# The mLSTM's queries held once per direction in tiles of 128 rows, with zeros in the other direction's half

## The chip, the cores and the metric

The kernel runs on one core of a Trainium2 chip. The metric is the device time of one execution in microseconds (us), lower is better, as the median of several executions. A profile of one execution gives the span from its first to its last instruction and what each engine did: TensorE (PE for its matmuls, PEld for its weight loads), VectorE (DVE), ScalarE (ACT), GpSimd (POOL), and SyncE's queue (SPq), which issues the transfers.

## The reference, cut to what matters

Two layers of a hybrid backbone run over 512 latent and 256 context tokens of 1024 features. In each layer a modulated RMSNorm feeds one input projection, and three mixers work side by side on it: a bidirectional mLSTM, grouped attention and a bidirectional gated delta net. Their outputs are gated, summed and projected, and a gated MLP follows. The change is in the mLSTM, which for each of 4 heads (64 features of q and k, 128 of v), for each direction and for chunks of tokens computes

```
s   = (q k^T) * exp(dlog - mt)                 within the chunk
num = s v + e_inter * (q C)                    C: the state before the chunk, [64, 128]
den = sum(s) + e_inter * (q n)                 n: [64]
h   = num / max(|den|, exp(-mt))
C, n <- decay * (C, n) + sum_s wk[s] k[s] (v[s], 1)
```

with q scaled by 64 ** -0.5 = 0.125. The forward and the backward h are added, normed over the head and gated. The last layer needs only the latent tokens.

## The kernel before

Tokens stand in six tiles of 128 (0 to 3 latent, 4 and 5 context); a tile is a chunk of the mLSTM. The tile framework of the kernel orders each engine's instructions by priorities and a timeline simulation, hands out slots of on-chip memory by tag (a tag has a fixed number of slots; a new tile of the tag waits until an old one is no longer read), and puts in all waits. `PLAN` names the order in which the parts of a layer are traced and their priorities: `P0`, `P1` and `g0`, `g1` are the delta net's projections and scans, `qp`, `ga` the attention, `mp` the mLSTM's projections, `ml` the mLSTM itself (function `mlstm`), and `mg` the gates of the merge, which are large products. In both layers `ml` is traced after `g1` and before `mg`; TensorE takes instructions of `g1`, `ml`, `mg` and of the modulation (`adp`, L467, 32 columns of the array) in turns, in one fixed sequence.

`gates` computes all decay factors. `X[:, 0]` are the factors e_inter; they are copied to `R2` (L839) and written as rows to DRAM, from where `row_bc` (L854) broadcasts rows over partitions.

`mlstm` has two parts. The first makes the states `U` of all tiles: rows 0 to 63 hold the forward direction's 64 features, rows 64 to 127 the backward direction's. The second, from L963 on, goes over the tiles (six in layer 0, four in layer 1), for each:

- `kT` (L964), 64 rows, and `qd` (L968), 128 rows with the same queries in both halves, are loaded from DRAM; both take slots of tag `b2`, which has seven and also serves `mb` (twice a tile) and `v`.
- `psS` (L972) is k times q for four heads, with 64 rows of the array.
- For each direction `mb` is loaded (L854), turned into decay weights (DVE L979, ACT L981) and multiplied by `psS` (DVE L982).
- `qd` is multiplied by 0.125 and by `e2`, the rows e_inter of the forward direction in the upper half and of the backward direction in the lower (L988, one DVE instruction over 128 x 512).
- For each pair of heads, direction and head a product with all 128 rows (L1002: decay weights times v) opens the sum in PSUM, and a product with 64 rows (L1004) adds the state's part. The forward direction uses rows 0 to 63 and the backward direction rows 64 to 127 of `qd` and `U`. The first tile of a direction has no state and no L1004.
- L1010 to L1037 divide, add the directions, norm, turn and gate, and store the tile as `m0y` or `m1y`; on GpSimd run `rsqrt` (L183) and L1035 there, and the memset of a column of `v` (L918).

An f32 product is two instructions (passes) on TensorE: layer 0 has 6 x 2 x 4 - 8 = 40 products of L1004 and layer 1 has 4 x 2 x 4 = 32. `merge` takes the delta net's output first, then the attention's, then the mLSTM's.

Of the kernel before, what the change touches and what calls it, by code (L numbers as in the profile page):

```python
# [13 lines left out]
ALU = mybir.AluOpType  # L14
AX = mybir.AxisListType

D = 1024
# [12 lines left out]
# columns of the input projection  # L30
# [5 lines left out]
# token tiles 0..3 are latent, 4 and 5 context; scan orders of the two directions  # L36
ORDER = ((4, 5, 0, 1, 2, 3), (5, 4, 3, 2, 1, 0))

# The mixers of each layer: the order in which their parts are traced, the priorities of the parts and of the weights
# (the long chains of small steps first, the large products in between), the PSUM of the context tokens in P1.  # L40
# P0, P1: projections of the delta net's pairs of heads, g0, g1: their scans; qp, ga: attention; mp, ml: mLSTM;
# cz, ao, mg: gates; n: from here on columns of the modulation in between.
# [51 lines left out]
class Kernel:  # L94
# [7 lines left out]
    # ---------------------------------------------------------------- pools  # L102
# [18 lines left out]
    # slots of the mixers' phase: a.. for the delta net, b.. for the others, gs for the projections  # L121
# [21 lines left out]
    # slots of the phase of the merge and the feed forward  # L143
# [12 lines left out]
    # PSUM banks: latent and context tokens of the large products, the delta net, the others  # L156
# [3 lines left out]
    def p0(self):  # L160
        """Banks of the latent tokens: those of the context tokens too where there are none."""
        self.turn = not self.turn
        return self.pb if self.spare and self.turn else self.pl
# [14 lines left out]
    # ---------------------------------------------------------------- small helpers  # L178
    def rsqrt(self, out, z, n, nm, who="n"):
        """out = z ** -0.5 for [128, n] float32 z (bit trick and Newton steps)."""  # L180
        nc = self.nc
# [18 lines left out]
    def split(self, h, l, x, eng=None):  # L200
        """x = h + l, both in float32r."""
# [5 lines left out]
    # ---------------------------------------------------------------- weights  # L207
    def wraw(self, src, nk, ncols, nm, slot=None):
        """raw weights [128, nk, ncols] from src rows (k p), columns given."""
# [17 lines left out]
    def gemm_fm(self, src, c0, ncols, nk, segs, done, nm):  # L227
        """Feature-major product: columns c0.. of src [nk*128, *] as stationary, tokens moving.
        segs: list of (token range, xh [128, nk, n], xl), latent first.
        done(block, [(psum, token range)]) takes the result."""  # L230
# [23 lines left out]
    def first_weights(self, src, c0, nk, nm, slot=None):  # L254
        """Weights for gemm_first."""
        h = l = None
# [879 lines left out]
    def attend_q(self, l, tt, tabs):  # L1136
# [7 lines left out]
        r = []  # L1144
# [769 lines left out]
```

## Time and profile before

| what | value |
|---|---|
| median of 3 runs | 2726.53 us (2725.04 to 2727.49) |
| span of the profiled execution | 2715.6 us, so that 10.9 us of the median lie outside the span |
| PE busy | 2663.0 us (98%) |
| DVE, ACT, POOL busy | 1573.4 us (58%), 998.5 us (37%), 235.0 us (9%) |
| chain that ended last | PE 88%, DMA 5%, DVE 3% |

No time other than the span is recorded for the profiled execution itself. A busy PE is not PE at its peak: the ends of matmuls are modelled, so the cost of a kind of product is read from the distance of starts, not from the busy time.

### The profile page before, as it was taken

To read this page: it belongs to the slowest core of one execution; us is meant where nothing else is said; L and a number is where in the kernel's file an instruction comes from. 1 tells how busy PE (TensorE), PEld (TensorE's weight loads), DVE (VectorE), ACT (ScalarE), POOL (GpSimd) and SP (SyncE) were. 2 spreads that over 40 slices of the span, in tenths; PEclk is the share of its full clock that TensorE was granted. 3 is DMA by queue.
4 is the path that set the end of the run, shared out by engine and by line. 5 is a ranking of instruction groups with operands and counts; after the bars stand their busy time and mean duration, and the time that the engine had idled before them with its cause. 6 is when DMAs were issued, how large, how long until landed. Compare 5 with 4: busy or idle time off the path is not lost.

```text
span 2715.6 us, 46016 instructions
## 1 busy us (share of the span) xinstructions
PE 2663.0 (98%) x18041; PEld 2261.6 (83%) x18041; DVE 1573.4 (58%) x3527; ACT 998.5 (37%) x2269; POOL 235.0 (9%) x234
## 2 busy tenths in 40 slices
PE   7999999999999999999999999999999999999999
PEld 5887988788888888888888899888877777888887
DVE  6775665756524655444444577867675646655555
ACT  5433354333322234232232254444633332433332
POOL 1000000000000410010010120000000003100000
PEclk9999999999999999999999999999998999999999
DMA  8354332556746423412212254422376675333332
GB/s 281 96 162 127 90 113 80 155 149 172 210 145 223 140 88 104 140 47 74 66 47 78 61 152 121 138 61 79 114 215 179 169 237 156 114 95 95 93 97 86
DMA packets 523466, 342.97 MB, mean 126 GB/s; under 512 B 48007, under 2 KB 488561, under 8 KB 522481
## 3 DMA queue, kind: packets, MB, share of 16 engines
q1 hardware_dynamic: 522961, 336.88, 42.2%
q8 instruction: 142, 2.33, 0.3%
q10 hardware_dynamic: 288, 3.15, 0.3%
q14 instruction: 75, 0.61, 0.1%
HBM read 283.92 MB, written 56.03 MB: 125 GB/s over the span
## 4 chain that ended last, share of the span: by engine, by line
PE 88%; DMA 5%; DVE 3%; ACT 1%; issue 1%; SPq 1%; POOL 0%; DVEq 0%; ACTq 0%; POOLq 0%
PE mg04p L249 2%; PE mg04p L250 2%; PE adp L467 2%; PE mg04p L248 2%; PE y0p L248 1%; PE y0p L250 1%; PE y0p L249 1%; PE mg14p L248 1%; PE mg14p L250 1%; PE mg14p L249 1%; PE y1p L248 1%; PE y0op L248 1%; PE y0op L250 1%; PE y0op L249 1%; PE y1p L249 1%
## 5 line engine op out<-in xcount | busy, mean ns | idle before, releaser
L1714 POOL TENSOR_TENSOR f0a<-f0a,f0g 128x768 f32<-128x768 f32 x22 | 40.7, 1848 | 486.8 <-DVE f0a L1702 486.8
L467 PE MATMUL adp<-ad,s 128*32 128x128 f32 x1280 | 65.5, 283 | 2.7 <-DVE cz0t L903 2.4
L1714 POOL TENSOR_TENSOR f1a<-f1a,f1g 128x512 f32<-128x512 f32 x22 | 28.5, 1294 | 315.4 <-DVE f1a L1702 284.4
L467 PEld LDWEIGHTS adp<-ad,s 128*32 128x32 f32 x1280 | 33.9, 110 | 26.0 <-issue 9.9
L1716 DVE TENSOR_TENSOR f0gl<-f0a,f0gh 128x768 fp32r<-128x768 f32 x22 | 21.1, 959 | 58.4 <-ACT f0gh L1715 58.4
L1715 ACT CAST f0gh<-f0a 128x768 fp32r<-128x768 f32 x22 | 18.3, 832 | 76.6 <-POOL f0a L1714 76.6
L1638 POOL TENSOR_TENSOR y0a<-y0a,y0g 128x768 f32<-128x768 f32 x16 | 33.0, 2062 | 129.9 <-DVE y0g L1635 127.6
L470 ACT COPY adr<-adp 128x128 f32<-128x128 f32 x80 | 21.2, 265 | 39.7 <-PE adp L467 39.3
L901 ACT ACTIVATE mg0t<-mg04p 128x512 f32<-128x512 f32 (+1 forms) x40 | 19.4, 486 | 38.5 <-PE mg04p L250 28.2
L1708 ACT ACTIVATE f0g<-f0g 128x768 f32<-128x768 f32 x22 | 18.5, 845 | 33.2 <-DVE f0g L1702 33.2
L1638 POOL TENSOR_TENSOR y1a<-y1a,y1g 128x512 f32<-128x512 f32 x16 | 23.9, 1494 | 78.3 <-DVE y1g L1635 78.3
L491 DVE TENSOR_REDUCE ada<-adc 128x2 f32<-128x8 f32 x80 | 12.9, 161 | 27.9 <-PE adc L489 27.6
L1635 DVE SCALAR_TENSOR_TENSOR y0g<-y0g,y0p 128x512 f32<-128x512 f32 (+1 forms) x32 | 17.4, 549 | 15.7 <-PE y0p L250 14.7
L1708 ACT ACTIVATE f1g<-f1g 128x512 f32<-128x512 f32 x22 | 13.8, 631 | 32.9 <-DVE f1g L1702 32.9
L979 DVE SCALAR_TENSOR_TENSOR m0mb<-m0mb,g0a,cst 128x128 f32<-128x128 f32 x48 | 14.0, 346 | 18.4 <-DMA m0mb<-g0rd 18.4
L489 PE MATMUL adc<-cst,adr 128*128 128x128 f32 x80 | 22.2, 278 | 0.4 <-ACT adr L470 0.4
L1659 DVE SCALAR_TENSOR_TENSOR hr<-y0op,y0gh,hr 128x512 f32<-128x512 f32 (+1 forms) x16 | 9.8, 615 | 21.0 <-PE y0op L250 21.0
L1002 PE MATMUL m0n<-m0vb,m0mb 128*128 128x129 f32 x96 | 19.1, 299 | 1.1 <-issue 1.1
L1611 DVE TENSOR_TENSOR y0l<-y0ld,y0h 128x768 fp32r<-128x768 f32 x12 | 13.0, 1093 | 12.2 <-ACT y0h L1610 12.2
L1734 DVE SCALAR_TENSOR_TENSOR hr<-f0d8p,ada,hr 128x512 f32<-128x512 f32 (+1 forms) x16 | 9.9, 618 | 15.7 <-PE f0d8p L250 15.7
L1734 DVE SCALAR_TENSOR_TENSOR hr<-f0d12p,ada,hr 128x512 f32<-128x512 f32 (+1 forms) x16 | 9.9, 618 | 15.7 <-PE f0d12p L250 15.7
L1734 DVE SCALAR_TENSOR_TENSOR hr<-f0d4p,ada,hr 128x512 f32<-128x512 f32 (+1 forms) x16 | 9.9, 618 | 15.7 <-PE f0d4p L250 15.7
(3922 smaller groups left out, 9921.5 us busy)
## 6 DMA issues: line engine op xcount, KB each, us to landing
ad<-ada_w SPq DMA_DIRECT2D x96, 512.0 KB, 4.0
mg04r<-w_in SPq DMA_DIRECT2D x20, 512.0 KB, 5.2
mg14r<-w_in SPq DMA_DIRECT2D x20, 512.0 KB, 5.1
y0g<-mg SPq DMA_DIRECT2D x24, 384.0 KB, 4.2
mg<-mg0t SPq DMA_DIRECT2D x24, 256.0 KB, 2.0
y0r<-w_branch SPq DMA_DIRECT2D x12, 512.0 KB, 3.9
mg<-mg1t SPq DMA_DIRECT2D x24, 256.0 KB, 4.3
y1r<-w_branch SPq DMA_DIRECT2D x12, 512.0 KB, 4.2
```

The lines of the kernel that those rows point to most:

```text
L248: nc.tensor.matmul(o, hv[:, k, :], xh[:, k, :], start=(k == 0), stop=False)
L249: nc.tensor.matmul(o, hv[:, k, :], xl[:, k, :], start=False, stop=False)
L250: nc.tensor.matmul(o, lv[:, k, :], xh[:, k, :], start=False, stop=(k == nk - 1))
L467: nc.tensor.matmul(ps[32 * j:32 * j + 32, 0:128], self.s32[:, 2 * k:2 * k + 32], raw[:, k, :], start=(k < 4), stop=(k >= 4), tile_position ...
L470: nc.scalar.copy(rw, ps[:, 0:128])
L489: nc.tensor.transpose(ps[:, 128:256], rw, self.ident)
L901: nc.scalar.activation(s, o, AF.Tanh, scale=0.5)
L1638: nc.gpsimd.tensor_tensor(out=a[:, :nt], in0=a[:, :nt], in1=gt[:, :nt], op=ALU.add)
L1708: nc.scalar.activation(a[:, :nt], a[:, :nt], AF.Silu)
L1714: nc.gpsimd.tensor_tensor(out=a[:, :nt], in0=a[:, :nt], in1=keep[b][:, :nt], op=ALU.mult)
L1716: nc.vector.tensor_tensor(out=gl[:, k, :nt], in0=a[:, :nt], in1=gh[:, k, :nt].bitcast(F32), op=ALU.subtract)
L1734: nc.vector.scalar_tensor_tensor(out=hv[:, a:b], in0=ps, scalar=self.ada[l][:, 40 + j, (a >= SEQ):(a >= SEQ) + 1], in1=hv[:, a:b], op0=ALU ...
```

## The change

Two persistent tiles `qz` of [128, 2, 4, 128] take turns for the tiles of tokens. Column block d holds the queries in direction d's half of the rows; the other half is set to zero once a layer, on GpSimd. So q of one direction is a full 128-row operand that is zero where `U` (and `kT`) hold the other direction. `kT` is loaded twice, into both halves of the rows, and the scores use `qd[:, 0]`, whose lower half is zero. The multiplication by e_inter moves from one DVE instruction to two GpSimd instructions on 64 rows, and the factor 0.125 into the copy in `gates`. The builder's `dynamic_dma_scratch_size` is set to 1024. The rest of the diff removes comments and docstrings.

```diff
@@ gates
-        nc.vector.tensor_copy(R2[:, 0:48], X[:, 0])
+        nc.vector.tensor_scalar(out=R2[:, 0:48], in0=X[:, 0], scalar1=0.125, scalar2=None, op0=ALU.mult)
@@ mlstm
+        qz = [self.P([128, 2, 4, 128], f"{nm}qz{i}", f"mqz{i}", 1) for i in range(2)]
+        for z in qz:
+            for d in range(2):
+                nc.gpsimd.memset(z[64 - 64 * d:128 - 64 * d, d], 0.0)
         for tt in range(nt // 128):
-            kT = self.b2([64, 4, 128], f"{nm}kTb{tt}")
-            nc.sync.dma_start(kT.rearrange("p (b u) t -> p b u t", u=2),
-                              self.ak[:, :, 128 * tt:128 * tt + 128].rearrange("b (u p) t -> p b u t", u=2))
-            qd = self.b2([128, 4, 128], f"{nm}qd{tt}")
+            kT = self.b2([128, 4, 128], f"{nm}kTb{tt}")
+            qd = qz[tt % 2]
             for d in range(2):
-                nc.sync.dma_start(qd[64 * d:64 * d + 64].rearrange("p (b u) t -> p b u t", u=2),
+                r = slice(64 * d, 64 * d + 64)
+                nc.sync.dma_start(kT[r].rearrange("p (b u) t -> p b u t", u=2),
+                                  self.ak[:, :, 128 * tt:128 * tt + 128].rearrange("b (u p) t -> p b u t", u=2))
+                nc.sync.dma_start(qd[r, d].rearrange("p (b u) t -> p b u t", u=2),
                                   self.aq[:, :, 128 * tt:128 * tt + 128].rearrange("b (u p) t -> p b u t", u=2))
...
-                nc.tensor.matmul(psS[:, 128 * h:128 * h + 128], kT[:, h, :], qd[0:64, h, :], start=True, stop=True)
+                nc.tensor.matmul(psS[:, 128 * h:128 * h + 128], kT[:, h, :], qd[:, 0, h, :], start=True, stop=True)
...
-            nc.vector.scalar_tensor_tensor(out=qd, in0=qd, scalar=0.125, in1=e2, op0=ALU.mult, op1=ALU.mult)
+            for d in range(2):
+                r = slice(64 * d, 64 * d + 64)
+                nc.gpsimd.tensor_tensor(out=qd[r, d], in0=qd[r, d], in1=e2[r], op=ALU.mult)
...
-                            nc.tensor.matmul(o, qd[r, h, :], U[r, prev[d][tt], h, :], start=False, stop=True)
+                            nc.tensor.matmul(o, qd[:, d, h, :], U[:, prev[d][tt], h, :], start=False, stop=True)
@@ build
-    nc = bacc.Bacc("TRN2", target_bir_lowering=False, num_devices=1)
+    nc = bacc.Bacc("TRN2", target_bir_lowering=False, num_devices=1,
+                   dynamic_dma_scratch_size=1024)
```

## Rows read from the trace of the kernel before

**Rows 1.** The page: the span's head, and the chain that ended last, by engine.

```profile
span 2715.6 us, 46016 instructions
...
PE 88%; DMA 5%; DVE 3%; ACT 1%; issue 1%; SPq 1%; POOL 0%; DVEq 0%; ACTq 0%; POOLq 0%
```

**Rows 2.** Busy time by stretch, the mLSTM's second part and after; clock share behind POOL.

```profile
680.00:720.00 40.00, 40.00 (x278) 32.64 (x276) 21.16 (x65) 16.47 (x47) 3.20 (x4) 1.00 0.79 227
780.00:830.00 50.00, 50.00 (x286) 43.61 (x285) 10.85 (x10) 14.60 (x22) 0.00 (x0) 1.00 0.60 206
...
2060.00:2100.00 40.00, 38.45 (x356) 30.05 (x344) 20.29 (x63) 13.10 (x35) 2.16 (x3) 0.83 0.56 157
```

**Rows 3.** Instructions by tile and line: the two products with 64 rows, both layers.

```profile
L1004 PE MATMUL m0n<-m0U,m0qd x80: 272/323/375, 625.3 to 763.0; 64*128 64x129 f32 x80
L1004 PE MATMUL m1n<-m1U,m1qd x64: 272/374/580, 2062.7 to 2162.2; 64*128 64x129 f32 x64
L972 PE MATMUL m0S<-m0qd,m0kTb x48: 272/272/373, 613.8 to 753.7; 64*128 64x128 f32 x48
```

**Rows 4.** PE in order of time: start, us, line, rows*columns, count.

```profile
629.07 0.49 PE L1002 MATMUL m0n<-m0vb,m0mb 128*128 128x129 f32 x2
629.49 0.49 PE L1004 MATMUL m0n<-m0U,m0qd 64*128 64x129 f32 x2
629.91 0.49 PE L1002 MATMUL m0n<-m0vb,m0mb 128*128 128x129 f32 x2
...
632.54 0.39 PE L1431 MATMUL c01op<-c01v,c01QE 128*128 128x128 f32 x2
...
632.99 0.39 PE L1431 MATMUL c01op<-c01v,c01QE 128*128 128x128 f32 x2
```

**Rows 5.** PE in order of time: two directions' L1004 side by side.

```profile
2153.95 0.49 PE L1002 MATMUL m1n<-m1vb,m1mb 128*128 128x129 f32 x2
2154.37 0.49 PE L1004 MATMUL m1n<-m1U,m1qd 64*128 64x129 f32 x4
2154.79 0.49 PE L1002 MATMUL m1n<-m1vb,m1mb 128*128 128x129 f32 x2
```

**Rows 6.** PE in order of time around the first scores.

```profile
613.48 0.39 PE L1433 MATMUL c01op<-c01S,c01qG 128*128 128x128 f32 x2
613.80 1.16 PE L972 MATMUL m0S<-m0qd,m0kTb 64*128 64x128 f32 x8
614.88 0.51 PE L249 MATMUL mg04p<-n00xl,mg04s5h 128*128 128x512 f32 x1
```

**Rows 7.** GpSimd's groups by line and form: busy us, mean ns, idle before.

```profile
L1638 POOL TENSOR_TENSOR y1a<-y1a,y1g 128x512 f32<-128x512 f32 x16 | 23.9, 1494 | 78.3 <-DVE y1g L1635 78.3
L1035 POOL TENSOR_TENSOR m0so<-m0so,m0anw 128x512 f32<-128x512 f32 x6 | 6.4, 1061 | 40.9 <-DVE m0so L1033 34.1 <-DMA mg<-mg0t 6.8
L1510 POOL MEMSET c01ix<- 96x1024 f32 x1 | 0.9, 950 | 0.0
L918 POOL MEMSET m0vb<- 128x4 f32 x6 | 0.6, 106 | 88.7 <-PE m0n L1002 66.4 <-PE m0pk L935 11.7 <-DMA m0mb<-g0rd 10.6
```

**Rows 8.** DVE and PE in order of time at the second tile, layer 0.

```profile
657.31 0.68 DVE L988 SCALAR_TENSOR_TENSOR m0qd<-m0qd,m0e 128x512 f32<-128x512 f32 x1
...
659.50 0.49 PE L1004 MATMUL m0n<-m0U,m0qd 64*128 64x129 f32 x4
```

**Rows 9.** PE at the start of layer 1's first tile, at the lower clock.

```profile
2062.21 0.54 PE L1002 MATMUL m1n<-m1vb,m1mb 128*128 128x129 f32 x2 [1.55 <-issue]
...
2065.88 0.63 PE L249 MATMUL mg14p<-n10xl,mg14s9h 128*128 128x512 f32 x1
2066.31 0.63 PE L250 MATMUL mg14p<-n10xh,mg14s9l 128*128 128x512 f32 x1
```

**Rows 10.** Layer 1's end of the mixers: what DVE waited for, and PE.

```profile
DVE c11on L1488: 7.5, 2
...
2203.72 0.50 PE L248 MATMUL mg10p<-n10xh,mg10s2h 128*128 128x512 f32 x1 [2.13 <-ACT mg1t L901]
```

More of the change, by code (lines that the diff above doesn't have):

```diff
@@ L995, in mlstm @@
                 for d in range(2):
-                    r = slice(64 * d, 64 * d + 64)
                     pn = self.pb(f"{nm}n{tt}_{hp}{d}")
```

## The prediction

> **What bounds the kernel now.** I read the page first: the span is 2715.6 us and the chain that ended last lies on TensorE for 88% of it [rows 1], so a saving counts if it shortens TensorE's sequence. I then looked by stretch at the place that the change touches. In the mLSTM's second part TensorE is busy without a gap (40.00 of 40.00 us), and behind it, between 780 and 830 us, still (50.00 of 50.00), because the gates' products `mg` are left over when the last tile is done [rows 2]. In layer 1 the stretch is nearly as full (38.45 of 40.00). The mLSTM's own latencies are therefore covered by other products; what counts is how long its instructions hold TensorE.
>
> The third view is TensorE in order of time, where the distance of starts tells what an instruction costs. In the delta net's scan two products alternate, all with 128 rows: from 632.54 to 632.99 us are two products, four passes, so 0.112 us a pass [rows 4]. In the mLSTM L1002 (128 rows) and L1004 (64 rows) alternate in the same way, into one bank with nearly the same columns (129 instead of 128), but from 629.07 to 629.91 four passes take 0.84 us instead of 0.45 [rows 4]. Nothing is waited for in those lines. What differs is the number of rows, so I read 0.39 us as the price of going from 128 rows to 64 and back, some 0.195 us a border.
>
> **What is removed: the borders.** L1004 has 80 passes in layer 0 and 64 in layer 1 [rows 3]. Followed through the whole timeline they stand in 52 stretches of two passes (28 and 24 by layer), as in rows 4, and 10 of four (6 and 4), as in rows 5; 52 x 2 + 10 x 4 = 144 = 80 + 64.
>
> - Stretches of two: 52 x 0.39 = 20.3 us.
> - Stretches of four: here the forward and the backward product stand side by side, and they share their time. From 2153.95 to 2154.79 us there are six passes in 0.84 us [rows 5], no more than four passes take with one product between [rows 4]. With 128 rows they can't share: six passes x 0.112 = 0.67 us. The gain is 0.17 us each, 10 x 0.17 = 1.7 us.
> - Scores: 48 passes for six tiles [rows 3], eight in a row. Up to the first product behind them 613.48 to 614.88 holds ten passes, 1.40 us instead of 1.12 [rows 6]; the rest of the second border falls on the product after that one, as the two borders of rows 4 do. Ten tiles x 0.39 = 3.9 us.
>
> The sum is 25.9 us, 14.3 of it in layer 0 (28 x 0.39 + 6 x 0.17 + 6 x 0.39) and 11.6 in layer 1. The number of passes and their columns stay. Eight passes with 64 rows take 1.08 us from 613.80 to 614.88, which is 8 x 0.112 and one border of 0.19 [rows 6]: a pass costs the same with 64 rows as with 128, so the zeros are free.
>
> A rule speaks against this. The Trainium skill, "TensorEngine Tiling (Array Packing)", section "When to Use Tiling", says that a contraction of at most 64 rows should be put into half the array, since two such products then run at once. By it alone each of the 72 products would cost half, and taking the halves away would cost 72 x 0.112 = 8.1 us instead of saving anything. The trace bears it out for the 20 products that stand in pairs [rows 5] and not for the 52 that stand alone between products of 128 rows; the same page's section "Key Properties" says that a change of mode drains the engine, which is what rows 4 show.
>
> **What is moved: the multiplication by e_inter.** DVE loses 0.68 us a tile [rows 8]. GpSimd gets two instructions on 64 x 512. No row has this form; the nearest with 128 x 512 took 1.06 us (one operand broadcast) and 1.49 us (two full ones) [rows 7], so a tile takes 2.1 to 3.0 us; 64 partitions need not be cheaper. If GpSimd starts when DVE did, it ends 1.4 to 2.3 us later. In the second tile DVE ended at 657.99 and L1004 began at 659.50 [rows 8], which leaves 1.5 us: TensorE would wait 0 to 0.8 us, over ten tiles 0 to 8 us. Against it: DVE does L988 in its queue behind other work, while GpSimd can begin once the scores have read the tile and `e2` is there; and DVE reaches the next weights 0.68 us sooner. GpSimd's own queue is the danger: the memset L918 sat 66.4 us in all behind L1002 of the tile before [rows 7], and what stands behind it waits too. But that wait comes from the seven slots of `b2`, of which a tile takes five now and four after, so the next tile's `v` gets its slot earlier. I take 1 us off for this, and for the few stretches next to L467, whose 32 columns keep a border.
>
> **What is added.** Four memsets of 64 x 512 a layer: 96 x 1024 took 0.95 us [rows 7], so about 0.5 us each, between 0 and 4 us in all; GpSimd's idle time hides them. One more load of 128 KB a tile: one issue on SPq's queue, ahead of `qd`, then weights and gates behind it; unhidden, some 0.6 us a tile if every scores' product waits for it, so 0 to 6 us. TensorE has `mg` to run meanwhile, and I take 0. The scaled copy in `gates` is one DVE instruction for one, two in the kernel: 0. Persistent tiles and the smaller scratch move addresses in on-chip memory and change what waits for which slot, and the order that the framework finds; I know no price for that and give it 5 us both ways.
>
> **Sum.** 25.9 - 1 = 24.9 us from a span of 2715.6; the 10.9 us outside the span stay. From the median of 2726.5 that gives 2702 us.
>
> **The rivals.**
>
> 1. *Layer 1 keeps its time.* Right behind the mixers the merge needs the delta net's last output. TensorE already waited 2.13 us there at 2203.72 [rows 10]. If that tail has its own length, a TensorE that arrives earlier only waits longer, and layer 1's 11.6 us shrink to nothing: 2726.5 - 13.3 = 2713. Against it: in that tail DVE waited 7.5 us for TensorE [rows 10], so the tail moves with TensorE. In layer 0 the `mg` products behind the mLSTM leave no such place [rows 2].
> 2. *The clock in layer 1.* The granted clock between 2060 and 2100 us was 0.83 on average [rows 2]: behind a wait of 1.55 us at 2062.21 TensorE ran at the lower of its two levels, 1.2 GHz, where a 512-column product stepped 0.43 us [rows 9]. A mean of 0.83 over 40 us is 13.6 us at half clock, in which 6.8 us of work at 2.4 GHz was done, so a fall that doesn't come would give up to 6.8 us more: 2695. The wait was for the decay weights, which stood behind L988 on DVE; moving that shortens it by 0.68 of 1.55 us. It may as well fall elsewhere. The Trainium skill's page "TensorE: Matmul & The Clock Gate", section "Part 1: The HAM clock gate", has a busy TensorE go back to full rate; nothing here tells whether this gap would still be long enough.
> 3. *It doesn't do what it says.* If the 0.39 us came from two operand streams taking turns in one bank, zeros would not help: 2726. Against it the delta net's products of rows 4, which also alternate in one bank, at 0.112 us.
> 4. *Slower: GpSimd paces TensorE.* The scaling stands in GpSimd's queue behind L918 or L1035 of another tile, and L1004 is next in TensorE's fixed sequence. Ten tiles share 25.9 us, so this decides once TensorE waits over 2.6 us in every tile; 4 us each (the two instructions at 3.0 us and one of 1.06 ahead of them) would give 2726.5 - 25.9 + 40 = 2741. Against it the slack of 1.5 us [rows 8] and the idle time ahead of GpSimd's instructions [rows 7].
>
> **How the numbers follow.** Forecast (2697 to 2708): 0.55. Rival 2 with the forecast (below 2697): 0.13. Rival 1 or a worse order of work (2708 to 2721): 0.20. Rival 3 or a gain lost elsewhere (within 0.2%, that is 5.5 us, which is about what a measurement can tell): 0.06. Rival 4: 0.06. The range 2695 to 2718 leaves out about 0.07 below and 0.15 above. Faster 0.88, same 0.06, slower 0.06.
>
> **What would show it.** L972 and L1004 with 128 rows; L1002 and L1004 alternating at 0.22 us per product, so 0.45 us where rows 4 have 0.84; no L1004 pair starting together; the same count of passes; the end of `mg` in layer 0 earlier by about 14 us and in layer 1 by about 25. I am wrong if L1004 has idle time before it that GpSimd ends, if the distance stays at 0.84, or if the wait of rows 10 grows by what was saved.

## The result and the profile after

The changed kernel took 2708.47 us (median of 4 runs, 2705.23 to 2712.51) beside 2725.78 us for the kernel before on the same chip: a ratio of 0.9942, 95% interval 0.9928 to 0.9957, or 17.3 us less. In two later comparisons (runs e2 and e8 below) the same kernel was 12.0 and 10.4 us faster than the one before. So it is faster by 0.3 to 0.6%. The 2708.47 us lie inside the range of 2695 to 2718, but just above the 2697 to 2708 that the prediction held most likely, and 10.4 to 17.3 us are less than the 24.9 us of its sum. One of the executions of run e12 below took 10477 us at a mean granted clock of 0.24; without it that run's median is 2711.19 us.

The page of the kernel after begins with the span, the busy time of its engines (of which the line with TensorE is shown) and, further down, the chain that ended last:

```profile
span 2710.7 us, 46057 instructions
...
PE 2640.8 (97%) x18041; PEld 2252.5 (83%) x18041; DVE 1576.0 (58%) x3517; ACT 1000.3 (37%) x2269; POOL 267.0 (10%) x262
...
PE 84%; DMA 7%; DVE 6%; ACT 1%; issue 1%; SPq 1%; POOL 0%; ACTq 0%; DVEq 0%; POOLq 0%
```

Two numbers of the page matter most. TensorE is busy for 2640.8 us instead of 2663.0, 22.2 less. And it is idle for 2710.7 - 2640.8 = 69.9 us instead of 2715.6 - 2663.0 = 52.6, 17.3 more. DVE's share of the chain went from 3% to 6% and DMA's from 5% to 7% [rows 1]. The spans of these two executions differ by only 4.9 us; that the idle time grew by as many us as the median fell is chance.

The saving is where it was expected. First, the products by line (count: shortest/median/longest ns, first and last start, form):

```profile
L1013 PE MATMUL m0n<-m0U,m0qz x80: 273/275/276, 631.3 to 767.4; 128*128 128x129 f32 x80
...
L1013 PE MATMUL m1n<-m1U,m1qz x64: 275/275/368, 2072.7 to 2156.4; 128*128 128x129 f32 x64
```

They have the counts of [rows 3], with 128 rows. In order of time on TensorE (start, us, line, rows*columns, count) the scores now stand without a border, and the two products alternate so:

```profile
620.38 0.39 PE L1442 MATMUL c01op<-c01S,c01qG 128*128 128x128 f32 x2
620.60 1.06 PE L980 MATMUL m0S<-m0qz,m0kTb 128*128 128x128 f32 x8
621.41 0.48 PE L249 MATMUL mg04p<-n00xl,mg04s5h 128*128 128x512 f32 x1
...
631.11 0.38 PE L1011 MATMUL m0n<-m0vb,m0mb 128*128 128x129 f32 x2
631.33 0.39 PE L1013 MATMUL m0n<-m0U,m0qz 128*128 128x129 f32 x2
631.55 0.39 PE L1011 MATMUL m0n<-m0vb,m0mb 128*128 128x129 f32 x2
```

From 631.11 to 631.55 are four passes in 0.44 us, where [rows 4] have 0.84; the ten passes up to the product behind the scores take 1.03 us, where [rows 6] have 1.40. The scaling on GpSimd came out between the bounds that [rows 7] gave, and the memsets at a little over half of the one there (groups: busy us, mean ns, idle before and what ended it):

```profile
L998 POOL TENSOR_TENSOR m0qz<-m0qz,m0e 64x512 f32<-64x512 f32 x12 | 15.4, 1282 | 151.9 <-DMA m0e<-g0rd 115.2 <-issue 20.8 <-PE m0S L980 15.9
...
L968 POOL MEMSET m0qz<- 64x512 f32 x4 | 2.2, 543 | 0.2
```

What is new is the idle time. The stretches of [rows 2], with PE's busy time second and the clock third from the end:

```profile
680.00:720.00 40.00, 37.08 (x254) 31.53 (x255) 21.81 (x72) 15.96 (x43) 7.97 (x10) 0.96 0.67 194
780.00:830.00 50.00, 50.00 (x283) 43.37 (x283) 11.60 (x11) 14.61 (x22) 1.96 (x1) 1.00 0.60 205
2060.00:2100.00 40.00, 35.63 (x528) 29.46 (x514) 26.41 (x80) 15.68 (x39) 6.47 (x7) 0.96 0.79 214
```

The stretch that had no gap now has 2.92 us of them, and the clock's low stretch of layer 1 is nearly gone (0.96 for 0.83) while PE waits longer there. TensorE's longest waits in the mLSTM's stretch of layer 0, 600 to 850 us (total us, times, longest):

```profile
PE mg04p L248 <- ACT mg0t L902: 3.4, 2, 3.1
PE c01vp L1426 <- DVE c01r L1422: 1.6, 1, 1.6
PE m0n L1011 <- issue: 1.2, 3, 0.7
```

and in that of layer 1, 2010 to 2240 us:

```profile
PE m1pt L1040 <- DVE m1hs L1034: 4.3, 3, 2.1
PE mg14p L250 <- issue: 2.2, 1, 2.2
PE mg10p L248 <- ACT mg1t L902: 1.5, 1, 1.5
```

Two of these waits, followed back. In layer 0, the 3.1 us: SyncE's queue issues the gate rows `m0mb`, DVE waits for them, ScalarE waits for DVE, and the eviction `mg0t` that `mg` needs stands behind that exponential in ScalarE's queue. The timeline of SPq, DVE, ACT and PE (in brackets: idle before, and what ended it):

```profile
674.22 0.55 SPq L855 DMA_DIRECT2D m0mb<-g0rd  x1
...
680.28 1.14 DVE L987 SCALAR_TENSOR_TENSOR m0mb<-m0mb,g0a,cst 128x128 f32<-128x128 f32 x4 [5.86 <-DMA m0mb<-g0rd]
...
681.50 0.63 ACT L989 ACTIVATE m0mb<-m0mb 128x512 f32<-128x512 f32 x1 [5.74 <-DVE m0mb L987]
682.03 0.58 ACT L902 ACTIVATE mg0t<-mg04p 128x512 f32<-128x512 f32 x1
...
682.67 0.50 PE L248 MATMUL mg04p<-n00xh,mg04s9h 128*128 128x512 f32 x1 [3.06 <-ACT mg0t L902]
```

So `mg`, which was to cover the mLSTM's latency, is itself held up by it. In layer 1, one of the three waits of `m1pt`: DVE again waits for the rows, and the sums of squares (L1031) stand behind that wait in DVE's queue, then GpSimd's power (L183), DVE's norm (L1034) and the transposes:

```profile
2110.97 1.14 DVE L987 SCALAR_TENSOR_TENSOR m1mb<-m1mb,g1a,cst 128x128 f32<-128x128 f32 x4 [2.96 <-DMA m1mb<-g1rd]
2112.03 0.16 DVE L1031 TENSOR_SCALAR m1ss<-m1ss 128x4 f32<-128x4 f32 x1
...
2112.33 1.01 POOL L183 TENSOR_TENSOR m1rs<-m1ss,mhalf 128x4 f32<-128x4 f32 x1 [5.73 <-DMA m1qz<-aq]
...
2113.38 0.69 DVE L1034 TENSOR_TENSOR m1hs<-m1hs,m1rs 128x512 f32<-128x512 f32 x1 [1.19 <-POOL m1rs L183]
...
2114.12 0.66 PE L1040 MATMUL m1pt<-cst,m1hs 128*128 128x128 f32 x4 [1.05 <-DVE m1hs L1034]
```

The row of GpSimd names a DMA as the releaser, but its operand `m1ss` was written at 2112.03 to 2112.19; that is what it waited for.

### The profile page after: what moved, and what is told of

The parts are those of the page before. It is cut to its first block, busy times and chain, and to the rows that moved or that the text cites. A ratio compares the mean times of both kernels' runs of the same rounds, so it can differ in the third digit from the quotient of the medians.

```text
span 2710.7 us, 46057 instructions
## 1 busy us (share of the span) xinstructions
PE 2640.8 (97%) x18041; PEld 2252.5 (83%) x18041; DVE 1576.0 (58%) x3517; ACT 1000.3 (37%) x2269; POOL 267.0 (10%) x262
## 3 DMA queue, kind: packets, MB, share of 16 engines
q8 instruction: 142, 2.33, 0.3%
## 4 chain that ended last, share of the span: by engine, by line
PE 84%; DMA 7%; DVE 6%; ACT 1%; issue 1%; SPq 1%; POOL 0%; ACTq 0%; DVEq 0%; POOLq 0%
PE mg04p L248 2%; PE mg04p L250 2%; PE mg04p L249 2%; PE adp L467 2%; PE y0p L248 1%; PE y0p L249 1%; PE y0p L250 1%; PE mg14p L248 1%; PE mg14p L250 1%; PE mg14p L249 1%; PE y1p L248 1%; PE y0op L248 1%; PE y0op L250 1%; PE y0op L249 1%; PE y1p L249 1%
## 5 line engine op out<-in xcount | busy, mean ns | idle before, releaser
L1725 DVE TENSOR_TENSOR f0gl<-f0a,f0gh 128x768 fp32r<-128x768 f32 x22 | 21.1, 958 | 61.4 <-ACT f0gh L1724 61.3
L1724 ACT CAST f0gh<-f0a 128x768 fp32r<-128x768 f32 x22 | 18.4, 835 | 80.0 <-POOL f0a L1723 80.0
L1717 ACT ACTIVATE f0g<-f0g 128x768 f32<-128x768 f32 x22 | 18.5, 846 | 32.9 <-DVE f0g L1711 32.9
L998 POOL TENSOR_TENSOR m0qz<-m0qz,m0e 64x512 f32<-64x512 f32 x12 | 15.4, 1282 | 151.9 <-DMA m0e<-g0rd 115.2
L987 DVE SCALAR_TENSOR_TENSOR m0mb<-m0mb,g0a,cst 128x128 f32<-128x128 f32 x48 | 14.1, 346 | 18.7 <-DMA m0mb<-g0rd 18.6
L1668 DVE SCALAR_TENSOR_TENSOR hr<-y0op,y0gh,hr 128x512 f32<-128x512 f32 (+1 forms) x16 | 9.8, 615 | 21.1 <-PE y0op L250 21.1
```

What stands on the lines that cost most here:

```text
L1717: nc.scalar.activation(a[:, :nt], a[:, :nt], AF.Silu)
L1725: nc.vector.tensor_tensor(out=gl[:, k, :nt], in0=a[:, :nt], in1=gh[:, k, :nt].bitcast(F32), op=ALU.subtract)
```

## The experiments

All ratios are to the kernel before as it was measured beside the run, with their 95% intervals. For each run the table has the page's busy and idle time of TensorE, and its idle time in the two mLSTM stretches together (600 to 850 and 2010 to 2240 us: 480 us less the busy time there). These are windows of fixed times, so they don't hold quite the same work in every run. Busy time is counted in us, so a stretch at the lower clock counts twice as long as the same work at the higher one.

| run | median us (ratio) | PE busy | PE idle | idle in the mLSTM stretches |
|---|---|---|---|---|
| before (profiled execution) | | 2663.0 | 52.6 | 9.8 |
| after (profiled execution) | 2708.47 (0.9942) | 2640.8 | 69.9 | 20.0 |
| e1 before, small scratch | 2723.11 (0.9999) | 2659.8 | 54.2 | 11.0 |
| e2 after again | 2710.24 (0.9962) | 2638.5 | 68.1 | 20.3 |
| e3 after, products on 64 rows | 2733.58 (1.0045) | 2673.4 | 55.3 | 8.8 |
| e4 after, scaling on DVE | 2716.17 (0.9984) | 2649.1 | 63.5 | 18.5 |
| e5 after, small scaling on ACT | 2714.47 (0.9982) | 2643.3 | 68.7 | 14.5 |
| e6 after, rows once a layer | 2695.38 (0.9909) | 2640.3 | 53.3 | 6.6 |
| e7 before, products grouped | 2706.17 (0.9951) | 2654.9 | 55.3 | 9.0 |
| e8 after, third time | 2710.69 (0.9966) | 2641.9 | 67.1 | 18.7 |
| e9 before, rows once a layer | 2725.50 (1.0016) | 2665.2 | 57.1 | 9.1 |
| e10 after, rows one tile ahead | 2724.28 (1.0012) | 2642.7 | 73.1 | 17.3 |
| e11 after, three query buffers | 2708.36 (0.9956) | 2637.9 | 64.5 | 16.8 |
| e12 after, rows on ACT's queue | 2712.02 (0.9960) | 2644.8 | 67.3 | 20.0 |

### e1: the smaller scratch alone

```diff
-    nc = bacc.Bacc("TRN2", target_bir_lowering=False, num_devices=1)
+    nc = bacc.Bacc("TRN2", target_bir_lowering=False, num_devices=1,
+                   dynamic_dma_scratch_size=1024)
```

> The kernel before with the smaller DMA scratch and nothing else; its instructions and their order are those of before. Theory A (part of the gain lies outside the span and comes from the scratch: the changed kernel's profiled run took 1.8 us more than its span, the kernel before some 10.9 us): 8 to 11 us faster than before, about 2716, with the span unchanged near 2714. Theory B (all of the gain is the mLSTM's): within 2 us of before, and the time outside the span stays near 11 us.

Measured: 2723.11 beside 2722.27 us, ratio 0.9999 (0.9984 to 1.0013). No effect of the scratch can be seen. In this run, as in every later one, the timed duration of the profiled execution (2715.83) is 1.8 us above its span (2714.0). So the "10.9 us outside the span" of the prediction do not exist: the profiled execution of the kernel before took 2715.6 + 1.8 = 2717.4 us, below the median.

### e2: the changed kernel beside the others

> The changed kernel once more, on the chip of its rivals and with a second profile. Both theories: 15 to 19 us faster than before, about 2708. If the 6.9 us by which its first profile was late before the mLSTM's second part began were chance, this profile has less; if they belong to the change, it has them again.

Measured: 2710.24 us, ratio 0.9962 (0.9949 to 0.9975), 12.0 us faster. It is the control for e3 and e4.

### e3: the changed kernel with its products on 64 rows

```diff
-   matmul(psS[...], kT[:, h, :], qd[:, 0, h, :], ...)
+   matmul(psS[...], kT[0:64, h, :], qd[0:64, 0, h, :], ...)
-   matmul(o, qd[:, d, h, :], U[:, prev[d][tt], h, :], ...)
+   matmul(o, qd[64 * d:64 * d + 64, d, h, :], U[64 * d:64 * d + 64, prev[d][tt], h, :], ...)
```

> The changed kernel with all products on 64 rows again: the scores use the upper halves, and L1013 the direction's half of the same tiles. Loads, memsets, GpSimd's scaling, slots and scratch stay. Borders theory: TensorE gets some 25.9 us of borders back, less what it now waits for in the mLSTM's stretches (about 9 us in the first profile): 10 to 24 us slower than the changed kernel, 2718 to 2732. Rival (borders cost nothing in the end, the gain is scratch and slots): within 4 us of the changed kernel.

Measured: 2733.58 us, ratio 1.0045 (1.0030 to 1.0061), 23.3 us slower than e2. The borders are back, four passes from 639.00 to 639.83:

```profile
638.68 0.39 PE L1011 MATMUL m0n<-m0vb,m0mb 128*128 128x129 f32 x2
639.00 0.49 PE L1013 MATMUL m0n<-m0U,m0qz 64*128 64x129 f32 x2
639.41 0.49 PE L1011 MATMUL m0n<-m0vb,m0mb 128*128 128x129 f32 x2
639.83 0.49 PE L1013 MATMUL m0n<-m0U,m0qz 64*128 64x129 f32 x2
```

In this order 68 of the 72 products stand alone and four in two stretches of two, and two tiles' scores are split, which makes 12 stretches of scores: 82 x 0.39 = 32.0 us of borders by the prediction's price. TensorE's busy time is 2673.4 - 2638.5 = 34.9 us above that of e2, part of it from the clock, which stood at its lower level for longer here (see below). But e2's idle time is 68.1 - 55.3 = 12.8 us above that of e3, so only 22.1 us of it show in the spans. And the idle time sits where the products are. The two stretches of e3:

```profile
600.00:850.00 250.00, 247.37 (x1609) 209.34 (x1608) 109.31 (x340) 79.92 (x219) 27.53 (x30) 1.00 0.61 180
2010.00:2240.00 230.00, 223.79 (x1654) 178.39 (x1653) 135.40 (x377) 77.59 (x198) 25.33 (x30) 0.99 0.71 205
```

They hold 8.8 us of idle time, e2's 20.3. This kernel has all the loads, memsets and GpSimd instructions of the change and waits no more than the kernel before. So the waits don't come from what the change adds by itself; they appear when TensorE gets through its own work sooner. e3 is 11.3 us slower than the kernel before although its mLSTM waits are the same: by the same prices 32.0 - 25.9 = 6.1 us of that are its ten more stretches and the pairs that no longer share the array, and the attention's stretch of layer 0 took 329 us where the kernel before had 322 (see e5).

### e4: the scaling back on DVE

```diff
-                nc.gpsimd.tensor_tensor(out=qd[r, d], in0=qd[r, d], in1=e2[r], op=ALU.mult)
+                nc.vector.tensor_tensor(out=qd[r, d], in0=qd[r, d], in1=e2[r], op=ALU.mult)
```

> The changed kernel with the two multiplications by the state's factor on DVE in place of GpSimd. Theory that GpSimd's queue gave part of the gain back (the norm's power of a tile waits behind the next tile's scaling, which waits for its loads): 3 to 8 us faster than the changed kernel, 2700 to 2705, and TensorE's waits for the normed rows (4.3 us in layer 1) go. Rival (loads set those waits): within 2 us; or DVE's two instructions of some 0.7 us a tile cost more than they free: 2 to 6 us slower.

Measured: 2716.17 us, ratio 0.9984 (0.9974 to 0.9994), 5.9 us slower than e2. The theory that GpSimd's queue costs 3 to 8 us falls. But the mean granted clock of the runs was 0.991 here and 0.994 in e2, which is some 8 us by an estimate (0.003 of 2712 us), more than the whole difference. So e4 doesn't show that DVE is the dearer place. The waits move: `m1pt` no longer waits, but others do, in layer 1 (2010 to 2240 us) with this list:

```profile
PE mg10p L248 <- ACT mg1t L902: 4.3, 1, 4.3
PE mg14p L248 <- DVE ada L491: 2.9, 1, 2.9
PE mg14p L250 <- issue: 2.6, 1, 2.6
```

### e5: a small scaling of the attention on ScalarE

In layer 0's attention, which the change doesn't touch, the kernel after lost 4 to 5 us (from the first `b0a4pq` to the last `ao00p` 325.9 us, 326.9 in e8, and 322.0 before). There a scaling of 128 x 2 numbers on DVE, L1204, met GpSimd's memsets. The timeline of DVE, POOL and PE in the kernel after:

```profile
499.27 2.28 DVE L1204 TENSOR_SCALAR b0a2nb<-b0a2nb 128x2 f32<-128x2 f32 x1
...
499.26 1.38 POOL L1529 MEMSET c01XT<- 128x1536 f32 x1 [58.14 <-DVE b0a2nb L1203]
500.58 0.95 POOL L1519 MEMSET c01ix<- 96x1024 f32 x1
...
502.42 0.85 PE L1215 MATMUL b0a2pp<-cst,b0a2P 128*128 128x128 f32 x4 [3.45 <-ACT b0a2P L1208]
```

```diff
-            nc.vector.tensor_scalar(out=nb, in0=nb if lat else mx[:, 0, :], scalar1=-0.125, scalar2=None, op0=ALU.mult)
+            nc.scalar.activation(nb, nb if lat else mx[:, 0, :], AF.Copy, scale=-0.125)
```

> The changed kernel with one edit: the 128x2 scaling of the attention's row maxima (L1204) on ScalarE instead of VectorE. Theory C (collision): in the changed kernel this scaling fell beside GpSimd's memset of the delta net's inverse and took 2.28 us instead of 0.17 (2.12 in its second profile), TensorE waited 3.5 to 3.9 us for it and its clock fell for 3.4 us after; without the collision the layer-0 attention stage falls from 326 us back to about 322 and the whole is 3 to 5 us faster than the changed kernel. Rival D (the stage is longer for another reason, the order of the queues): the stage stays at 326 us and the total within 1.5 us of the changed kernel, since 30 small scalings more on ScalarE are 30 x 0.2 = 6 us of an engine that is idle most of the stage. Rival E: ScalarE is where the next wait comes from, and the total rises by 2 to 6 us.

Measured: 2714.47 us, ratio 0.9982 (0.9971 to 0.9993), 3.8 us slower than e8, which was measured beside it. The wait itself shrank, as TensorE's row shows (a second wait of 0.47 us follows):

```profile
502.12 0.65 PE L1215 MATMUL b0a2pp<-cst,b0a2P 128*128 128x128 f32 x4 [1.96 <-ACT b0a2P L1208]
```

But the attention's stretch kept its length (326.9 us, as in e8): the edit also moved other instructions of DVE and ScalarE there, and layer 1 got a wait of 4.3 us for `mg1t`. Theory C's wait is shown; that the stretch hangs on it is not. Rival D fits its length, rival E the total.

### e6 and e9: the gate rows loaded once a layer

e6 is the changed kernel with this edit, e9 the kernel before with the same one and the small scratch. Both use the wrong rows for all tiles but the first; they show what the loads cost and are no kernels to keep.

```diff
+        raw = self.P([128, 4, 128], f"{nm}mraw", "mraw", 1)
+        self.row_bc(raw, 0, 0, 0, 0, 0, 4)
         for tt in range(nt // 128):
...
-                self.row_bc(mb, 0, 0, d, tt, 0, 4)
-                    nc.vector.scalar_tensor_tensor(out=mb[:, h, :], in0=mb[:, h, :], scalar=G["a"][:, i:i + 1],
+                    nc.vector.scalar_tensor_tensor(out=mb[:, h, :], in0=raw[:, h, :], scalar=G["a"][:, i:i + 1],
```

> The changed kernel without the twelve-odd loads of the gate rows per layer inside the mLSTM's loop: one load per layer into its own buffer serves all tiles and directions, so that the exponents of all tiles but the first come from the wrong rows (the loads are left out; every other operation is there). Theory F (latency chain): the layer-0 mLSTM gave back some 10 of its 14 us in waits of TensorE, because the new tile's gate rows are issued late on SyncE behind a wait and land 6 us later; without these loads the waits of layer 0 fall, and first score to last mg04p falls from 186 us towards 175 to 180, that is 5 to 10 us faster. Rival G (the waits come from GpSimd's scaling and ScalarE's queue, not from the loads): the stage stays within 2 us of 186. In layer 1 (123 us) both expect no more than 3 us, since the waits there stand behind GpSimd's small power of the means (L183).

> The kernel before, with the same work left out as in the run of the changed kernel with one load of the gate rows per layer (the loads of the gate rows inside the loop are left out, the exponents of all tiles but the first come from the wrong rows). Theory F2 (the change is worth its borders, about 23 us, wherever the mLSTM doesn't wait for rows): this kernel gains only its own small waits, 0 to 8 us, over the kernel before, so that the changed kernel without the loads (2695) is 18 to 26 us faster than this one (this one 2713 to 2721). Rival J (the loads cost both kernels alike, the gain of the change is some 11 us whatever waits there are): this kernel too is some 15 us faster than the kernel before, near 2706, and the difference between the two without loads stays 10 to 12 us.

Measured: e6 2695.38 us, ratio 0.9909 (0.9895 to 0.9924), 15.3 us faster than e8. e9 2725.50 us, ratio 1.0016 (1.0002 to 1.0030), not faster than the kernel before. So leaving out the loads gives the kernel before nothing and the changed kernel 15 us, and without them the change is worth 0.0107 x 2721 = 29 us. Rival J falls, and F2 is right in kind. Its 18 to 26 us look too low, but some 6 of the 29 us go with the clock: its mean over the runs was 0.994 in e6 and 0.992 in e9. The two mLSTM stretches of e6:

```profile
600.00:850.00 250.00, 249.10 (x1693) 219.51 (x1692) 120.27 (x345) 81.86 (x218) 26.98 (x29) 1.00 0.62 185
2010.00:2240.00 230.00, 224.27 (x1628) 185.30 (x1627) 139.23 (x356) 78.85 (x191) 30.97 (x29) 0.99 0.70 202
```

and those of e9:

```profile
600.00:850.00 250.00, 248.43 (x1638) 211.24 (x1627) 113.55 (x344) 80.51 (x219) 12.94 (x18) 1.00 0.60 177
2010.00:2240.00 230.00, 222.46 (x1590) 177.87 (x1586) 134.37 (x369) 75.12 (x188) 11.01 (x17) 0.98 0.67 192
```

Their idle times are 6.6 and 9.1 us, while e8, with the loads, has 18.7. The page's busy time falls from 2665.2 to 2640.3, by 24.9 us, and the idle time falls too, from 57.1 to 53.3: -28.7 us in all, and 29 were measured. Both theories of e6 expected no more than 3 us of layer 1, and rival G nothing anywhere; the larger part came in layer 1. The stages themselves separate this from the rest of the kernel. Layer 0's goes from the first score to the last `mg04p`, layer 1's to the last `mg14p`:

| run | layer 0 | layer 1 | attention, layer 0 |
|---|---|---|---|
| before, e1 | 189.0, 191.4 | 132.6, 132.6 | 322.0, 321.2 |
| after, e2, e8 | 185.9, 185.8, 181.3 | 122.8, 122.9, 123.7 | 325.9, 326.0, 326.9 |
| e9 (before, without the loads) | 188.4 | 129.3 | 325.9 |
| e6 (after, without the loads) | 177.7 | 113.5 | 324.4 |

With the loads the change makes the two mLSTM stages together 13 to 19 us shorter, without them 317.7 - 291.2 = 26.5 us. The kernel before does gain from their absence, 4 to 6 us in these stages, but e9 lost about as much in the attention. There L1204 met the memsets (see e5) as in the changed kernel, though of the change e9 has only the scratch:

```profile
498.94 1.38 POOL L1521 MEMSET c01XT<- 128x1536 f32 x1 [58.57 <-DMA c01dn<-c01XT]
...
499.35 1.88 DVE L1196 TENSOR_SCALAR b0a2nb<-b0a2nb 128x2 f32<-128x2 f32 x1
```

(L1196 is L1204 in that kernel.) In e6 it took 0.17 us. So some 2.5 of the 15.3 us lie in the attention (326.9 less 324.4) and not in the stages that wait for the rows. The order of all engines also moved with the edit, so the rest is that of the kernel without the loads, not of each wait.

### e7: the kernel before with its products grouped

Another way to fewer borders: 64 rows are kept, but for a pair of heads the four 128-row products come first and then the 64-row ones of both directions side by side.

```diff
+                pns = [self.pb(f"{nm}n{tt}_{hp}{d}") for d in range(2)]
                 for d in range(2):
...
                     for hh in range(2):
-                        nc.tensor.matmul(o, Ps[d][:, h, :], v[:, h, :], start=True, stop=first)
-                        if not first:
-                            nc.tensor.matmul(o, qd[r, h, :], U[r, prev[d][tt], h, :], start=False, stop=True)
+                        nc.tensor.matmul(pns[d][:, 129 * hh:129 * hh + 129], Ps[d][:, h, :], v[:, h, :], start=hh == 0,
+                                         stop=hh == 1 and tt not in prev[d])
+                for hh in range(2):
+                    h = 2 * hp + hh
+                    for d in range(2):
+                        r = slice(64 * d, 64 * d + 64)
+                        if tt in prev[d]:
+                            nc.tensor.matmul(pns[d][:, 129 * hh:129 * hh + 129], qd[r, h, :], U[r, prev[d][tt], h, :],
+                                             start=False, stop=hh == 1)
...
```

> The kernel before, with its 64-row products kept, but for each pair of heads the four 128-row products first (one accumulation group for a bank) and then the 64-row products of both directions, forward and backward side by side; nothing is loaded, scaled or cleared that the kernel before doesn't. Theory A (a border of 128 and 64 rows costs 0.195 us, a pair of two directions shares the array): the stretches of 64-row products fall from 76 to some 35 to 40, and more of them run in pairs, so 36 to 41 stretches x 0.39 = 14 to 16 us, and up to 5 us from pairs side by side, against a pair's waits of 0 to 5 us: 10 to 20 us faster than the kernel before, without any of the changed kernel's new waits. Rival B (the changed kernel gained from its 128 rows as such, not from fewer borders): within 3 us of the kernel before. Rival H (the order moves with the edit, and a longer wait for both directions' P eats it): slower than the kernel before by 0 to 10 us.

Measured: 2706.17 us, ratio 0.9951 (0.9935 to 0.9966), 14.9 us faster than the kernel before. Counted through the timeline, the stretches of 64 rows in the mLSTM fell from 72 (62 of L1004 and ten of scores) to 43: 29 x 0.39 = 11.3 us. That the rest comes from pairs that share is likely, but was not separated. In TensorE's order of time, six passes of each kind stand together:

```profile
661.15 0.83 PE L999 MATMUL m0n<-m0vb,m0mb 128*128 128x129 f32 x6
661.91 0.71 PE L1006 MATMUL m0n<-m0U,m0qd 64*128 64x129 f32 x6
```

The next product starts at 662.55, so these six passes take 0.64 us, as long as four alone with a border before them (4 x 0.112 + 0.195). Its idle time in the mLSTM stretches is 9.0 us, little less than before (9.8). Beside it the changed kernel (e8) took 2710.69 us (ratio 0.9966, 0.9954 to 0.9978): the grouped kernel's median is 4.5 us lower, and the intervals overlap. So the change is not shown to be faster than grouping, which has none of its memory, loads and memsets. Rivals B and H fall.

### e8: the changed kernel a third time

> The changed kernel once more, beside the other kernels of this call: 10 to 18 us faster than the kernel before. Theory C expects the attention's 128x2 scaling to take about 2 us beside the memset again, and the layer-0 attention stage to last 326 us; if it's chance, the stage lasts 322 us and the total is 4 us less.

Measured: 2710.69 us, 10.4 us faster than before. The scaling L1204 took 2.19 us beside the memset again, and the attention's stretch 326.9 us, so it isn't the chance of one execution. In e1, whose order is that of the kernel before, the scaling took 0.17 us and the stretch 321.2 us. But it is no property of the change either: e7 and e9 have it too (2.33 and 1.88 us; 327.2 and 325.9 us).

### e10, e11, e12: three ways to have the rows earlier

e10 gives the rows four buffers and issues their loads a tile ahead; e11 has a third pair of query buffers, since the queries' load stands before the rows' in SyncE's queue; e12 issues the rows' loads from ScalarE.

```diff
@@ e10
...
+            if tt + 1 < nmb:
+                load_mb(tt + 1)
...
-                mb = self.b2([128, 4, 128], f"{nm}mb{tt}{d}")
-                self.row_bc(mb, 0, 0, d, tt, 0, 4)
+                mb = mbs.pop((tt, d))
@@ e11
-        qz = [self.P([128, 2, 4, 128], f"{nm}qz{i}", f"mqz{i}", 1) for i in range(2)]
+        qz = [self.P([128, 2, 4, 128], f"{nm}qz{i}", f"mqz{i}", 1) for i in range(3)]
-            qd = qz[tt % 2]
+            qd = qz[tt % 3]
@@ e12
...
-                self.row_bc(mb, 0, 0, d, tt, 0, 4)
+                self.row_bc(mb, 0, 0, d, tt, 0, 4, eng=nc.scalar)
```

> The changed kernel, complete, with the gate rows of a tile in four buffers of their own and loaded one tile ahead of their use. Theory F (the row loads' latency is what TensorE waits for): the waits of layer 0's mLSTM go as they did without the loads, stage from first score to last mg04p 176 to 180 us instead of 181 to 186, layer 1's 114 to 120 instead of 123, in all 5 to 14 us faster than the changed kernel. Rival K (it was the traffic of 0.25 MB per load or SyncE's queue, not the time of issue): within 2 us of the changed kernel, or slower, since the loads are still issued behind the queries' load that waits for a buffer.

> The changed kernel, complete, with three pairs of query buffers instead of two. Theory L (the queries' load waits for a buffer that is freed two tiles later, and SyncE's queue holds the gate rows' loads behind it): with a third buffer those loads are issued earlier, the waits of layer 0 and 1 shrink, 4 to 10 us faster than the changed kernel. Rival M (the load order follows the end of the scaling and other waits, not the buffer): within 2 us of the changed kernel; one more memset on GpSimd is 0.54 x 2 us at the start.

> The changed kernel, complete, with the 128-row loads of the gate rows issued by ScalarE instead of SyncE; the same bytes, into the same buffers, on another queue. Theory F3 (the rows are late because they stand in SyncE's queue behind the loads of the queries that wait for their buffer): the time comes near that of the kernel without these loads, 2695 to 2703, 8 to 15 us faster than the changed kernel, with the waits of the mLSTM gone from both layers. Rival K2 (the traffic of 0.25 MB a load, which competes with the weights for the DMA engines, or the latency of some 6 us itself): the traffic stays, so the time stays within 3 us of the changed kernel's 2710. Rival N (ScalarE waits in order for the buffers that it loads into, and its other work comes late): slower than the changed kernel by 2 to 10 us.

Measured: e10 2724.28 us (1.0012, 0.9998 to 1.0025); e11 2708.36 us (0.9956, 0.9940 to 0.9972); e12 2712.02 us (0.9960, 0.9943 to 0.9978). None recovers what e6 shows. Theory F's 5 to 14 us, L's 4 to 10 and F3's 8 to 15 didn't come; M and K2, within 2 and 3 us of the changed kernel's 2710, fit. e10 tells nothing about the rows: with it the order of layer 0 changed so much that the attention's stretch took 343 us instead of 326. e11 and e12 tell that neither the queries' buffer nor SyncE's queue alone is the cause: DVE's waits for the rows of layer 0 and 1 are 17.1 and 7.5 us in e11, 16.8 and 7.8 in e12, and in the changed kernel

```profile
DVE m0mb L987 <- DMA m0mb<-g0rd: 18.6, 7, 5.9
...
DVE m1mb L987 <- DMA m1mb<-g1rd: 8.9, 4, 5.1
```

The kernel before has nearly the same sums, 18.4 us in 9 waits and 9.2 in 6. They were there all along, and TensorE had work to cover them: in e9, without them, its two stages were only 4 to 6 us shorter.

## Why the prediction was right and where it was wrong

**The borders: right in kind, a little high in size.** Four passes take 0.44 us where they took 0.84, and without the loads the two stages are 26.5 us shorter, beside the sum of 25.9. The busy time of TensorE fell by 22.2 us in the first profile, 24.5 in e2's and 21.1 in e8's, by 24.9 between e9 and e6, and by 34.9 against e3, where the same prices give 32.0. These figures also hold the clock. With the time at the lower clock counted by half, an estimate from the granted clock in the traces, before and e1 have 2646 to 2648 us of work and after, e2 and e8 2627 to 2629, a fall of 18 to 21 us, and e3 lies 27 us above e2. So the borders are worth some 20 to 26 us; where the rest of the 25.9 went no run shows. A pass costs the same with zeros in half its rows (0.11 us from 631.11 to 631.55). Rival 3 falls. The Trainium skill's advice for half arrays, "TensorEngine Tiling (Array Packing)", section "When to Use Tiling", is borne out by e7 for products that find a partner in the other half (six passes in 0.64 us).

**The cover: wrong, and this is the step that failed.** That the time came out in the range all the same is in part luck: the clock in layer 1, for which the sum had nothing, gave some of the loss back (see the rivals below). The prediction's first part took from [rows 2] that "the mLSTM's own latencies are therefore covered by other products; what counts is how long its instructions hold TensorE", and the sum priced all waits, of GpSimd, loads and order, at -1 us in total. Measured, TensorE's idle time grew by 14.5 to 17.3 us over the three profiles of the change, 9 to 10.5 of them in the mLSTM's stretches. A stretch without gaps shows that latency was covered at that speed. It doesn't show by how much. The reading that fits: the rest of a tile's chain (row load, DVE, ScalarE, DVE, GpSimd, DVE) didn't get shorter while TensorE's work became some 2 to 2.6 us shorter a tile, and then the waits of DVE for its rows, present before, reached TensorE. e3 shows it from one side (all of the change but the rows of the products: 8.8 us idle), e6 and e9 from the other (no row loads: the two stages gain 26.5 us instead of 13 to 19). The other 5 to 7 us of new idle time lie outside the mLSTM, some 2 of them in the attention of layer 0, whose stretch grew by 4 to 5 us. That lies within the 5 us both ways that the prediction gave to a new order of work.

**GpSimd: the mechanism of rival 4 is seen but doesn't decide.** `m1pt` waits behind L183, 4.3 us in all; with the scaling on DVE that wait goes and the kernel is not faster (e4). The scaling took 1.28 us, inside the bounds of 1.06 and 1.49.

**The additions: nothing seen.** Memsets of 0.54 us, one more load, the copy and the scratch: e1 and e3 show no idle time from them in the mLSTM's stretches (11.0 and 8.8 us, 9.8 before).

**The span.** The "10.9 us outside" are 1.8; the rest is the distance of the profiled execution from the median. The forecast subtracted from the median, so this didn't move it. But that one execution was faster than the median, and so are the stages read from it; e1, the same program but for the scratch, has a profile of 2715.8 us and a median of 2723.

**The rivals of layer 1.** The wait of [rows 10] is 1.5 us instead of 2.13, and layer 1's stage became 8.9 to 9.8 us shorter, so rival 1 falls. Rival 2, which had a chance of 0.13 and no place in the sum, came about in part: the clock between 2060 and 2100 us was 0.96 for 0.83, by the prediction's own reckoning 5.2 us of work at the higher clock (6.8 less 1.6), about half of what layer 1's stage gained in the first profile. The time below 2697 didn't come, since the waits described above took it back. The medians stand at different clocks too: over the runs the mean granted clock was 0.992 for the kernel before beside e2 and 0.994 for e2, some 5 of its 12.0 us by an estimate (0.002 of 2710 us). Whether the change or chance raised it no run separates. The end of `mg` was not 14 us earlier in layer 0: from the first score it takes 185.9 us in the first profile and 181.3 in e8's, 189.0 before. In layer 1 it came 9 to 10 us sooner after the first score, of 11.6 forecast.

**Open.** Which property of the row loads would have to change: their bytes, their latency (medians of 5.0 us in layer 0 and 6.3 in layer 1 in the kernel after, 4.5 and 5.5 before), or the time at which the framework issues them. The sum of DVE's waits for them is no measure of the loss: in e5 it fell to 9.6 and 5.3 us, and the two stages, 183.4 and 129.6 us, were no shorter than in e8. Nor is it settled how much of the 4 to 5 us in the layer-0 attention belongs to the collision of L1204 and how much to the order around it.

## What to carry to other kernels

A stretch in which the bound engine has no gap proves cover only up to the time that you take out of it: before counting a saving on that engine in full, list the other engines' waits in the stretch (here 18 and 9 us of DVE waiting for rows), since these can surface when the engine gets faster. When products of half the array's rows alternate with full ones, count the borders, 0.39 us per stretch here; grouping them saved 14.9 us beside 10.4 for padding, with no new loads or memsets. And check each edit by one that undoes only its core, and compare by stages, since the order of everything else, and with it the clock, may move.

## What the runs showed of the hardware that was not expected

A DVE instruction on 128 x 2 numbers that takes 0.16 us took 1.87 to 2.33 us in nine runs (2.28, 2.12, 2.19 and 2.33 in after, e2, e8 and e7) when it began close to the first of two GpSimd memsets of 1.38 and 0.95 us, from 0.05 us ahead of it to 0.42 us behind; it ended about when the second did. In before, e1 and e6, where it began 0.44, 0.30 and 0.14 us ahead, it took 0.17 us. The Trainium skill, "SBUF — State Buffer", section "SBUF: two separate sides", describes a port pair that GpSimd and some kinds of DVE instruction lock for a whole instruction, so that the other fully blocks. These rows agree in that DVE lost the memsets' whole time, and they show the loss over two memsets in a row; that this lock is the cause no run here shows, and in e7 it was the DVE instruction that began first, by 0.05 us.
